# A hybrid FNet/Hyena encoder layer: z scaled behind later transposes, first spectra loaded during the filters, two units' spectra stored once and copied in DRAM

## The chip, the core and the metric

One Trainium2 chip, of which the kernel uses one core. A core has five engines with queues of their own: TensorE (PE: matrix products; its weight loads, PEld, run beside them), VectorE (DVE), ScalarE (ACT), GpSimd (POOL), and SyncE (SP), which here only starts DMA transfers. ACT starts some transfers too. Every queue is worked off in order; an instruction that waits holds all behind it on its engine. Engines wait for one another through semaphores. The metric is the device time of one launch in microseconds (us), lower is better.

## The reference, cut to what matters

```python
def reference(x, ...):                        # x: 1 x 2048 x 1024, float32, one layer
    h = rmsnorm(x, g_mix)
    p = h @ w_in                              # 1024 -> 2048 columns
    u_f, u_h = p[..., :512], p[..., 512:]
    y_f = rmsnorm(fourier_mix(u_f), g_fourier)     # Re(FFT2) over positions and 64 channels, 8 groups
    y_h = rmsnorm(hyena_mix(u_h, ...), g_hyena)
    x = x + concatenate([y_f, y_h]) @ w_out
    a = relu(rmsnorm(x, g_mlp) @ w_fc1) ** 2       # 1024 -> 4096
    return rmsnorm(x + a @ w_fc2, g_final)

def implicit_filters(...):                    # a small sine network over positions
    h = (hidden(positions) @ w_out) * decay   # 2 orders x 2 directions x 512 channels
    k = both directions joined to 4096 taps   # tap 0: forward + backward
    return k * rsqrt(sum(k * k) + EPS)

def hyena_mix(u, ...):
    x1, x2, v = split(short_conv(u))
    z = v
    for n, gate in enumerate((x1, x2)):       # rfft, product with the filter's spectrum, irfft
        z = gate * (irfft(rfft(z) * rfft(k[:, n])) + z * long_d[n])
    return z
```

## The kernel before

The stages follow each other: the input projections with short convolution (gates x1 and x2 until about 237 us, the Fourier group and v until about 408), `filters` (408 to 598, with the Fourier mixing in its first part), `hyena` (598 to about 800), the output projection, and the two large products of the MLP, which take more than half of the time. Matrix products of the projections and of the MLP are made in three passes over high and low parts. Transforms over positions are two stages of small matrix products with a DVE transpose between them.

**`filters` (L533).** Eight units `Unit(i)` make the spectra of eight filters of 128 channels: `ct = i // 2` is the channel block, `n = i % 2` the order. A loop of 44 steps (L675) is a pipeline over the units. Unit u multiplies out its taps in steps 4u to 4u+3: PE writes `pk` (L578), DVE multiplies by the decay into `k` (L583). For k = 0 ACT copies the tap in the middle to `lag0` (L592), DVE adds it to tap 0 (L593); for every k, ACT squares (L597) into `sqr` or, the first time, into `acc`, and POOL sums the squares (L599, folds L601, L602). In steps 4u+5 and 4u+6 the sum goes through PE (`psum_k`, L607) to the scales and to the skip term. The first stage of the transform is in steps 4u+7 to 4u+10 (PE L648, DVE transposes `Gk` L652), the second in 4u+12 to 4u+15 (PE L657, ACT copies into `ks` L660, and one store to DRAM a step, L664). A store writes the same 512 KB twice, for the two halves of the partitions of the later loads: 1024 KB. `ks` has three buffers.

In steps 0 to 10 the 16 first products of the Fourier mixing (L490, each followed by a DVE transpose `Gf`, L474) and then its 9 groups `rows(i)` (L494) are mixed in. `rows` makes the negative sines `neg` on ACT (L497) from the table `ff`; the table of the first group, `ff0`, is loaded at the start of the stage (L185). Of unit 0's four decay loads (L552), all are issued by ACT; those of later units by SP.

z, the input of the first Hyena order, is loaded from DRAM in steps 24 to 27 (L711) and multiplied by `norms`, the product of both orders' scales, from step 28 on (L715, 16 instructions). The framework's scheduler orders each engine's queue by priority, so instructions can stand earlier than the program text says.

**`hyena` (L719).** Eight blocks, first order (n = 0) of four channel blocks, then second order. A block takes `first` (PE L760, transposes), `second(q)` for eight q (PE L767, product with the spectrum `ks` on DVE and POOL, L773 to L775), `inverse` (PE L783), `turn`, `gate`; three blocks overlap. `spectrum(q)` (L737) loads 512 KB (L746); for q = 0 a small ACT copy moves row 64 (L749) and two POOL memsets clear two rows (L751). The first four spectra of block 0 are loaded at the stage's start (L805). Block i reads the unit with the same (n, ct): blocks 6 and 7 read units 5 and 7.

`behind(later, first)` (L202) puts instructions behind another one in the queue of the same engine, with no semaphore. `ordered` does that for PE, so that PE's order in the filters is that of the program text. A DMA takes one of eight semaphores in turn and is not issued before the transfer that had it last (eight transfers back) has landed.

The lines that matter in the order of the filters' loop are these:

```python
            if 0 < step < 32:
                units[u].generate(k)
...
            if 0 <= u < 8:
                units[u].stage1(r)
...
            if step in LOAD:
...
                nc.sync.dma_start(zzs[0][:, :, cs], gd[0][:, :, cs])
            j, q = divmod(step - 28, 4)
            if j >= 0:
                z = zzs[0][:, 4 * q : 4 * q + 4, 128 * j : 128 * j + 128]
                nc.vector.tensor_mul(z, z, norms[:, j : j + 1, :].broadcast_to([P, 4, 128]))
```

Of the kernel before, what the change touches and what calls it, by code (L numbers as in the profile page):

```python
# [134 lines left out]
def hybrid_block(ctx: ExitStack, tc: tile.TileContext, A, out):  # L135
# [203 lines left out]
    line = []  # L339
# [144 lines left out]
    def fourier(fp, uf, e1f, ffs):  # L484
# [8 lines left out]
        def rows(i):  # L493
# [3 lines left out]
            nc.scalar.mul(neg, ffs[i][:, :, 1], -1.0)  # L497
# [35 lines left out]
    def filters(ctx, tp, fp, gp, zp, zzs, norms, emb, wo, e1k, f2, dk8, tabs, fourier_steps):  # L533
# [7 lines left out]
        class Unit:  # L541
# [3 lines left out]
            def decay(self, k):  # L545

                if k < 2:
                    decs[k] = fp.tile([P, 8, 128], F32, tag="dec", name="dec", bufs=2)
                elif k == 2:
                    two = tp.tile([P, 2, 8, 128], F32, tag="dec2", name="dec2")  # L550
                    decs[2], decs[3] = two[:, 0], two[:, 1]
                d = (nc.scalar if self.i == 0 else nc.sync).dma_start(decs[k], A["decay"][self.ct][:, 8 * k : 8 * k + 8, :])  # L552
                if self.i == 0:
                    behind([d], line[0])
# [26 lines left out]
            def multiply(self, k, p, first=None):  # L581
# [7 lines left out]
                if k == 0:  # L589
                    zero, end = self.k[0:1, :, 0, :], self.k[32:33, :, 0, :]  # L590
                    lag0 = fp.tile([1, 128], F32, tag="lag0", name="lag0", bufs=2).rearrange("p (c j) -> p c j", c=8)
                    nc.scalar.copy(lag0, end)  # L592
                    nc.vector.tensor_add(zero, zero, lag0)  # L593
                    nc.vector.memset(end, 0.0)
# [43 lines left out]
            def stage1(self, r):  # L638
# [10 lines left out]
                for c in range(2):  # L649
                    src = p[:, :, 256 * c : 256 * c + 256].rearrange("p a (l c e) -> p c e a l", c=8, e=2)  # L650
                    dst = self.G.rearrange("p c (a f) e -> p c e a f", a=2)[:, 16 * r + 8 * c : 16 * r + 8 * c + 8]
                    nc.vector.transpose(dst, src)  # L652

            def stage2(self, q):
                p = pa("pk2")
                for j in range(4):
                    ordered(nc.tensor.matmul(p[:, 128 * j : 128 * j + 128], lhsT=f2[:, 4 * q + j, :], rhs=self.G[:, :, 4 * q + j], start=True, stop=True))  # L657
                if q % 2 == 0:
                    self.ks = sp[0].tile([P, 8, 128], F32, tag="ks", name="ks", bufs=3)
                nc.scalar.copy(self.ks[:, 4 * (q % 2) : 4 * (q % 2) + 4, :], p.rearrange("p (f c) -> p f c", f=4))  # L660
                if q % 2:

                    dst = kd[self.ct][self.n].rearrange("h p s x -> (p s) h x")[:, :, 512 * q - 512 : 512 * q + 512]
                    nc.sync.dma_start(dst, self.ks.rearrange("p (h f) c -> p h (f c)", h=1).broadcast_to([P, 2, 1024]))  # L664
# [9 lines left out]
        LOAD = {24: 0, 25: 1, 26: 2, 27: 3}  # L674
        for step in range(44):  # L675
# [21 lines left out]
            if 0 <= u < 8:  # L697
                units[u].stage1(r)
# [13 lines left out]
            j, q = divmod(step - 28, 4)  # L712
            if j >= 0:
                z = zzs[0][:, 4 * q : 4 * q + 4, 128 * j : 128 * j + 128]
                nc.vector.tensor_mul(z, z, norms[:, j : j + 1, :].broadcast_to([P, 4, 128]))  # L715
# [3 lines left out]
    def hyena(hp, wp, rp, zz, e1, b1, f2, a2, work):  # L719
# [6 lines left out]
        class Block:  # L726
# [9 lines left out]
            def spectrum(self, q):  # L736

                if self is blocks[7] and q > 3:
# [3 lines left out]
                    ks = self.room[:, q - 4]  # L742
                else:
                    ks = hp.tile([P, 2, 4, 128], F32, tag="ks", name="ks", bufs=4)
                src = kd[self.ct][self.n].rearrange("h p s x -> (h p) s x")[:, :, 512 * q : 512 * q + 512]
                nc.sync.dma_start(ks.rearrange("p s f c -> p s (f c)"), src)  # L746
# [58 lines left out]
        blocks = [Block(n, ct) for n in range(2) for ct in range(4)]  # L805
        for k in range(4):
            blocks[0].ahead[k] = blocks[0].spectrum(k)

# [3 lines left out]
        for i in range(8):  # L812
            cur, old, older, new = (blocks[j] if 0 <= j < 8 else None for j in (i, i - 1, i - 2, i + 1))
            for q in range(8):
# [28 lines left out]
                if new:  # L843
                    for c in FIRSTS[q]:
                        new.first(c)
        old, older = blocks[7], blocks[6]
# [705 lines left out]
```

## Time and profile before

| | us |
|---|---|
| three timed runs | 2271.7, 2274.6, 2276.61 |
| their median | 2274.6 |
| profiled execution | 2276.27 |
| its span in the trace | 2274.5 |
| PE busy in the span | 2204.1 |

Busy time by stage, from the windows of the trace:

| stage | window, us | PE | DVE | ACT | POOL | clock | DMA share |
|---|---|---|---|---|---|---|---|
| gates x1, x2 | 0 to 237 | 220.45 | 202.78 | 125.93 | 98.22 | 1.00 | 0.58 |
| Fourier group, v | 237 to 408 | 171.00 | 116.58 | 30.66 | 50.38 | 0.99 | 0.78 |
| filters | 408 to 598 | 172.82 | 123.46 | 88.08 | 83.50 | 0.96 | 0.77 |
| hyena | 598 to 800 | 195.20 | 154.31 | 118.91 | 125.14 | 0.99 | 0.79 |

A row of a timeline gives the start and the duration of an instruction (or of several like it, with their count after an x), the engine (ACTq and SPq are the queues that start transfers), the line, the operation, what is written and read, and in brackets the idle time before it with the instruction that ended it. A row of the waits gives the waiting instruction, what it waited for, the time in all, how often, and the longest. Clock is the share of TensorE's full clock that was granted; the DMA share is the busy share of the core's 16 DMA engines.

### The profile page before, as it was taken

To read this page: it belongs to the slowest core of one execution; us is meant where nothing else is said; L and a number is where in the kernel's file an instruction comes from. 1 tells how busy PE (TensorE), PEld (TensorE's weight loads), DVE (VectorE), ACT (ScalarE), POOL (GpSimd) and SP (SyncE) were. 2 spreads that over 40 slices of the span, in tenths; PEclk is the share of its full clock that TensorE was granted. 3 is DMA by queue.
4 is the path that set the end of the run, shared out by engine and by line. 5 is a ranking of instruction groups with operands and counts; after the bars stand their busy time and mean duration, and the time that the engine had idled before them with its cause. 6 is when DMAs were issued, how large, how long until landed. Compare 5 with 4: busy or idle time off the path is not lost.

```text
span 2274.5 us, 34533 instructions
## 1 busy us (share of the span) xinstructions
PE 2204.1 (97%) x12881; PEld 1800.7 (79%) x12881; DVE 1470.5 (65%) x2196; ACT 1074.3 (47%) x1788; POOL 768.9 (34%) x583
## 2 busy tenths in 40 slices
PE   8999899898999989998999999999999999999998
PEld 6888788576788858887888878888888888888886
DVE  6999667677487764456444466444466666866667
ACT  6545211354465654456555565555533333533333
POOL 3434232464276601246555556555300000000000
PEclk9999999999999999999999999999999999999999
DMA  8535887578977755657444474444498766866631
GB/s 272 177 134 173 297 300 256 188 257 305 368 247 219 235 158 167 199 181 247 158 153 151 152 249 167 153 153 152 140 352 324 241 194 194 305 191 197 188 119 74
DMA packets 296505, 477.00 MB, mean 210 GB/s; under 512 B 17349, under 2 KB 141455, under 8 KB 292113
## 3 DMA queue, kind: packets, MB, share of 16 engines
q1 hardware_dynamic: 290097, 458.29, 60.4%
q10 hardware_dynamic: 6240, 16.51, 2.1%
q8 instruction: 101, 1.65, 0.3%
q14 instruction: 67, 0.55, 0.1%
HBM read 305.17 MB, written 168.00 MB: 208 GB/s over the span
## 4 chain that ended last, share of the span: by engine, by line
PE 85%; DVE 4%; DMA 4%; ACT 3%; POOL 2%; issue 2%; ACTq 0%; SPq 0%; DVEq 0%; POOLq 0%
PE p2u L210 5%; PE p2u L212 5%; PE p2u L211 5%; PE p1u L212 5%; PE p1u L210 5%; PE p1u L211 5%; PE pu L212 4%; PE pu L211 4%; PE pu L210 4%; PE p2v L210 3%; PE p2v L212 3%; PE p2v L211 3%; PE pk L657 2%; PE p1v L210 2%; PE pz L760 2%; PE p1v L212 2%
## 5 line engine op out<-in xcount | busy, mean ns | idle before, releaser
L196 ACT CAST qahm<-ra 128x1024 fp32r<-128x1024 f32 x110 | 115.9, 1054 | 346.5 <-PE p2u L211 172.0
L197 DVE TENSOR_TENSOR qalm<-ra,qahm 128x1024 fp32r<-128x1024 f32 x110 | 134.7, 1224 | 153.7 <-ACT qahm L196 152.1
L1324 POOL TENSOR_TENSOR acc<-acc,gfin 128x512 f32<-128x512 f32 x4 | 5.1, 1278 | 631.6 <-DMA out<-acc 624.5
L211 PE MATMUL pu<-wl,xh 128*128 128x512 f32 x512 | 201.2, 393 | 6.9 <-DVE wl L197 6.5
L210 PE MATMUL pu<-wh,xh 128*128 128x512 f32 x512 | 203.7, 398 | 1.0 <-ACT wh L199 1.0
L212 PE MATMUL pu<-wh,xl 128*128 128x512 f32 x512 | 201.1, 393 | 1.5 <-DVE xl L197 1.5
L211 PE MATMUL p2u<-qblm,qahm 128*128 128x512 f32 x504 | 196.1, 389 | 0.0
L210 PE MATMUL p2u<-qbhm,qahm 128*128 128x512 f32 x504 | 195.8, 389 | 0.0
L212 PE MATMUL p2u<-qbhm,qalm 128*128 128x512 f32 x504 | 195.8, 389 | 0.0
L197 DVE TENSOR_TENSOR qblm<-rb,qbhm 128x1024 fp32r<-128x1024 f32 x110 | 134.0, 1218 | 1.1 <-ACT qbhm L196 0.9
L405 POOL TENSOR_TENSOR acc<-acc,cw 128x512 f32<-128x512 f32 x45 | 59.9, 1330 | 201.5 <-DVE acc L382 198.1
L196 ACT CAST ahm<-s 128x512 fp32r<-128x512 f32 x124 | 76.7, 621 | 98.5 <-PE p1v L211 53.7
L197 POOL TENSOR_TENSOR alm<-W,ahm 128x512 fp32r<-128x512 f32 x63 | 88.5, 1405 | 94.8 <-ACT ahm L196 94.8
L211 PEld LDWEIGHTS pu<-wl,xh 128*128 128x128 f32 x512 | 96.9, 189 | 28.5 <-DVE wl L197 6.9
L196 ACT CAST qbhm<-rb 128x1024 fp32r<-128x1024 f32 x110 | 115.3, 1049 | 3.3 <-DMA rb<-in_w_fc 2.1
L212 PEld LDWEIGHTS pu<-wh,xl 128*128 128x128 f32 x512 | 96.8, 189 | 22.9 <-DVE xl L197 3.0
L210 PEld LDWEIGHTS pu<-wh,xh 128*128 128x128 f32 x512 | 97.0, 189 | 22.2 <-ACT wh L199 1.8
L210 PEld LDWEIGHTS p2u<-qbhm,qahm 128*128 128x128 f32 x504 | 94.6, 188 | 20.1 <-issue 0.3
L212 PEld LDWEIGHTS p2u<-qbhm,qalm 128*128 128x128 f32 x504 | 94.6, 188 | 19.6
L211 PEld LDWEIGHTS p2u<-qblm,qahm 128*128 128x128 f32 x504 | 94.6, 188 | 19.6
L210 PE MATMUL p1u<-bm,ahm 128*128 128x512 f32 x252 | 99.5, 395 | 7.2 <-ACT ku L1186 7.2
L196 ACT CAST ahm<-W 128x512 fp32r<-128x512 f32 x94 | 57.7, 617 | 98.8 <-PE p1u L211 98.8
(376 smaller groups left out, 6153.3 us busy)
## 6 DMA issues: line engine op xcount, KB each, us to landing
W<-in_w_fc SPq DMA_DIRECT2D x66, 512.0 KB, 4.6
spec<-ks SPq DMA_DIRECT2D x32, 1024.0 KB, 5.7
ks<-spec SPq DMA_DIRECT2D x64, 512.0 KB, 4.7
rb<-td SPq DMA_DIRECT2D x64, 512.0 KB, 9.3
ra<-a1m SPq DMA_DIRECT2D x56, 512.0 KB, 3.6
ra<-a0m SPq DMA_DIRECT2D x54, 512.0 KB, 3.7
rb<-in_w_fc SPq DMA_DIRECT2D x46, 512.0 KB, 10.7
f<-in_w_fc SPq DMA_DIRECT2D x16, 1024.0 KB, 7.6
```

The lines of the kernel that those rows point to most:

```text
L196: nc.scalar.copy(hi, src)
L197: (eng or nc.vector).tensor_sub(lo, src, hi)
L210: a = nc.tensor.matmul(o, lhsT=lh, rhs=rh, start=start, stop=False, skip_group_check=more)
L211: nc.tensor.matmul(o, lhsT=lh, rhs=rl, start=False, stop=False, skip_group_check=more)
L212: return a, nc.tensor.matmul(o, lhsT=ll, rhs=rh, start=False, stop=stop, skip_group_check=more)
L405: nc.gpsimd.tensor_add(m1, m1, cw[:, 3, :])
L657: ordered(nc.tensor.matmul(p[:, 128 * j : 128 * j + 128], lhsT=f2[:, 4 * q + j, :], rhs=self.G[:, :, 4 * q + j], start=True, stop=True))
L760: nc.tensor.matmul(p[:, 256 * sp : 256 * sp + 256], lhsT=e1[:, sp, :], rhs=zz[:, :, lo : lo + 16], start=True, stop=True)
L1324: nc.gpsimd.tensor_mul(acc[i][:, c], acc[i][:, c], gfin[:, c])
```

## The change

There are five edits. (1) `neg` is put behind unit 0's lag copy in ACT's queue. (2) Of unit 0's decay loads the last two (`dec2`) are issued by SP instead of ACT. (3) z is scaled in steps 30 to 37, two instructions a step, and each is put behind the transposes of its step in DVE's queue. (4) The first four spectra of block 0 are loaded into a tile of their own, `ks4`, with a high priority and behind unit 3's last store in SP's queue, which is issued in step 27; the repair of q = 0 goes with them. (5) Units 5 and 7 store their spectra once (512 KB a store); the second half is written by eight copies from DRAM to DRAM, `doubled`, in blocks 1 and 2 of the hyena stage.

```diff
--- before.py
+++ after.py
@@ -336,7 +336,13 @@
                 w[h, k] = hi, lo
         return w
 
-    line = []
+    line, acts, fetched, stored = [], [], [], []
+    SINGLE = (5, 7)
+
+    def doubled(i, q):
+
+        both = kd[i // 2][i % 2].rearrange("h p s x -> h (p s) x")[:, :, 1024 * q : 1024 * q + 1024]
+        behind([nc.sync.dma_start(both[1], both[0])], fetched[0])
 
     def project(ip, fx, cps, sets, uf):
 
@@ -494,7 +500,7 @@
 
             n, p = len(groups[i]), pa("pf2")
             neg = fp.tile([P, 2, P], F32, tag="neg", name="neg", bufs=2)[:, 0:n]
-            nc.scalar.mul(neg, ffs[i][:, :, 1], -1.0)
+            behind([nc.scalar.mul(neg, ffs[i][:, :, 1], -1.0)], acts[0])
             for s, f in enumerate(groups[i]):
                 co, si, ns = ffs[i][:, s, 0], ffs[i][:, s, 1], neg[:, s]
                 a, b = p[:, 256 * s : 256 * s + 132], p[:, 256 * s + 132 : 256 * s + 256]
@@ -549,8 +555,8 @@
                 elif k == 2:
                     two = tp.tile([P, 2, 8, 128], F32, tag="dec2", name="dec2")
                     decs[2], decs[3] = two[:, 0], two[:, 1]
-                d = (nc.scalar if self.i == 0 else nc.sync).dma_start(decs[k], A["decay"][self.ct][:, 8 * k : 8 * k + 8, :])
-                if self.i == 0:
+                d = (nc.scalar if self.i == 0 and k < 2 else nc.sync).dma_start(decs[k], A["decay"][self.ct][:, 8 * k : 8 * k + 8, :])
+                if self.i == 0 and k < 2:
                     behind([d], line[0])
 
             def generate(self, k):
@@ -589,7 +595,7 @@
                 if k == 0:
                     zero, end = self.k[0:1, :, 0, :], self.k[32:33, :, 0, :]
                     lag0 = fp.tile([1, 128], F32, tag="lag0", name="lag0", bufs=2).rearrange("p (c j) -> p c j", c=8)
-                    nc.scalar.copy(lag0, end)
+                    acts.append(nc.scalar.copy(lag0, end))
                     nc.vector.tensor_add(zero, zero, lag0)
                     nc.vector.memset(end, 0.0)
                 for q in range(2):
@@ -649,7 +655,8 @@
                 for c in range(2):
                     src = p[:, :, 256 * c : 256 * c + 256].rearrange("p a (l c e) -> p c e a l", c=8, e=2)
                     dst = self.G.rearrange("p c (a f) e -> p c e a f", a=2)[:, 16 * r + 8 * c : 16 * r + 8 * c + 8]
-                    nc.vector.transpose(dst, src)
+                    last = nc.vector.transpose(dst, src)
+                return last
 
             def stage2(self, q):
                 p = pa("pk2")
@@ -660,8 +667,11 @@
                 nc.scalar.copy(self.ks[:, 4 * (q % 2) : 4 * (q % 2) + 4, :], p.rearrange("p (f c) -> p f c", f=4))
                 if q % 2:
 
-                    dst = kd[self.ct][self.n].rearrange("h p s x -> (p s) h x")[:, :, 512 * q - 512 : 512 * q + 512]
-                    nc.sync.dma_start(dst, self.ks.rearrange("p (h f) c -> p h (f c)", h=1).broadcast_to([P, 2, 1024]))
+                    n = 1 if self.i in SINGLE else 2
+                    dst = kd[self.ct][self.n][0:n].rearrange("h p s x -> (p s) h x")[:, :, 512 * q - 512 : 512 * q + 512]
+                    d = nc.sync.dma_start(dst, self.ks.rearrange("p (h f) c -> p h (f c)", h=1).broadcast_to([P, n, 1024]))
+                    if self.i == 3:
+                        stored[:] = [d]
 
         units = [Unit(i) for i in range(8)]
         decs, both, sp = {}, [], []
@@ -672,6 +682,7 @@
         SOLO = 11
         FOURIER = (4, 4, 4, 4, 2, 1, 1, 1, 1, 2, 1)
         LOAD = {24: 0, 25: 1, 26: 2, 27: 3}
+        SCALE = {30 + 2 * j + h: [(j, 2 * h), (j, 2 * h + 1)] for j in range(4) for h in range(2)}
         for step in range(44):
             if step == SOLO:
                 yield
@@ -695,7 +706,7 @@
                 units[u].generate(k)
             u, r = divmod(step - 7, 4)
             if 0 <= u < 8:
-                units[u].stage1(r)
+                flipped = units[u].stage1(r)
             u, q = divmod(step - 5, 4)
             if 0 <= u < 8 and q == 0:
                 units[u].scales()
@@ -709,10 +720,9 @@
                 if not zzs:
                     zzs.append(zp.tile([P, NT, 512], F32, tag="zz", name="zz"))
                 nc.sync.dma_start(zzs[0][:, :, cs], gd[0][:, :, cs])
-            j, q = divmod(step - 28, 4)
-            if j >= 0:
+            for j, q in SCALE.get(step, ()):
                 z = zzs[0][:, 4 * q : 4 * q + 4, 128 * j : 128 * j + 128]
-                nc.vector.tensor_mul(z, z, norms[:, j : j + 1, :].broadcast_to([P, 4, 128]))
+                behind([nc.vector.tensor_mul(z, z, norms[:, j : j + 1, :].broadcast_to([P, 4, 128]))], flipped)
         yield
 
 
@@ -740,10 +750,14 @@
                     if q == 4:
                         self.room = rp.tile([P, 4, 2, 4, 128], F32, tag="W", name="ks4")
                     ks = self.room[:, q - 4]
+                elif self is blocks[0] and q < 4:
+                    if q == 0:
+                        self.room = rp.tile([P, 4, 2, 4, 128], F32, tag="W", name="ks4")
+                    ks = self.room[:, q]
                 else:
                     ks = hp.tile([P, 2, 4, 128], F32, tag="ks", name="ks", bufs=4)
                 src = kd[self.ct][self.n].rearrange("h p s x -> (h p) s x")[:, :, 512 * q : 512 * q + 512]
-                nc.sync.dma_start(ks.rearrange("p s f c -> p s (f c)"), src)
+                fetched[:] = [nc.sync.dma_start(ks.rearrange("p s f c -> p s (f c)"), src)]
                 if q == 0:
 
                     nc.scalar.copy(ks[64:65, 0, 0, :], ks[64:65, 1, 0, :])
@@ -803,9 +817,11 @@
         LAST = ((0,), (1, 2), (3, 4), (5, 6), (7,))
         FIRSTS = ((0, 1), (2, 3), (4,), (5,), (6,), (7,), (), ())
         blocks = [Block(n, ct) for n in range(2) for ct in range(4)]
+        with tc.high_priority(offset=4000):
+            for k in range(4):
+                blocks[0].ahead[k] = blocks[0].spectrum(k)
+                behind(fetched, stored[0])
         for k in range(4):
-            blocks[0].ahead[k] = blocks[0].spectrum(k)
-
             nc.sync.dma_start(a2[:, 8 * k : 8 * k + 8], A["a2"][:, 8 * k : 8 * k + 8])
         for c in range(8):
             blocks[0].first(c)
@@ -843,6 +859,8 @@
                 if new:
                     for c in FIRSTS[q]:
                         new.first(c)
+                if i in (1, 2) and q % 2:
+                    doubled(SINGLE[i - 1], q // 2)
         old, older = blocks[7], blocks[6]
         for q in range(8 - LAG, 8):
             old.inverse(q)
```

PE's queue is the same in both programs. Three places of the other queues follow. In ACT's queue at the start of the filters before, the four loads of `dec` and `dec2` stand ahead of the copy of `longd`, and the two `neg` ahead of `lag`:

```order
L462 ACTIVATE uf<-pu_3563,nw_s 128x512
L552 DMA dec<-in_decay 128x1024 x2
L552 DMA dec_3622<-in_decay 128x1024 x2
L539 COPY longd<-plongd 128x8
L497 ACTIVATE neg<-ff_3612 128x128
L497 ACTIVATE neg<-ff 128x256
L592 COPY lag_3674<-k 1x128
L597 ACTIVATE sqr<-k 128x512
L597 ACTIVATE acc<-k 128x512
```

and of the change:

```order
L468 ACTIVATE uf<-pu_3563,nw_s 128x512
L558 DMA dec<-in_decay 128x1024 x2
L545 COPY longd<-plongd 128x8
L598 COPY lag_3674<-k 1x128
L603 ACTIVATE sqr<-k 128x512
L503 ACTIVATE neg<-ff_3612 128x128
L503 ACTIVATE neg<-ff 128x256
L603 ACTIVATE acc<-k 128x512
```

Two loads have left ACT, the lag copy and one square stand ahead of `neg`, and `acc`, which POOL's sums begin with, stands behind it.

In DVE's queue around step 24 the scaling of z (`zz<-zz,norms`) stood between the transposes `Gk` and the decay products `k` before (the last three rows are of step 24):

```order
L583 TENSOR_TENSOR k<-pk,dec_4723 128x8x8x16
L715 TENSOR_TENSOR zz<-zz,norms 128x4x128 x2
L652 STREAM_TRANSPOSE Gk<-pk_5319 128x8x2x32 x2
L715 TENSOR_TENSOR zz<-zz,norms 128x4x128 x2
L583 TENSOR_TENSOR k<-pk,dec 128x8x8x16
L593 TENSOR_TENSOR k<-k,lag_5380 1x8x16
```

In the change the same transposes (of `pk_5319`) have none beside them, and the first scaling stands in step 30, behind its transposes (the first two rows below):

```order
L658 STREAM_TRANSPOSE Gk<-pk_5833 128x8x2x32 x2
L725 TENSOR_TENSOR zz<-zz,norms 128x4x128 x2
L589 TENSOR_TENSOR k<-pk,dec_5307 128x8x8x16
L658 STREAM_TRANSPOSE Gk<-pk_5903 128x8x2x32 x2
L725 TENSOR_TENSOR zz<-zz,norms 128x4x128 x2
L658 STREAM_TRANSPOSE Gk<-pk_5930 128x8x2x32 x2
```

All 16 scalings have moved behind the transposes of steps 30 to 37. In SP's queue of the change, the four loads of the first spectra (`ks_6229`, the tile `ks4`) stand between the stores of unit 3 (`spec_63`) and those of unit 4 (`spec_64`); before, the first of them stood behind all stores:

```order
L672 DMA spec_63<-ks 128x2x1024
L722 DMA zz<-gates_57 128x16x128
L672 DMA spec_63<-ks 128x2x1024
L760 DMA ks_6229<-spec_60 128x2x512 x4
L672 DMA spec_64<-ks 128x2x1024 x4
L717 DMA f2h<-in_f 128x1024 x2
L672 DMA spec_65<-ks 128x1024
```

and ACT's queue of the change has the repair of q = 0 in step 28, between step 27's copies into `ks` and unit 7's lag copy:

```order
L667 COPY ks<-pk_5627 128x512
L667 COPY ks<-pk_5634 128x512
L763 COPY ks_6229<-ks_6229 1x128
L598 COPY lag_5677<-k 1x128
L603 ACTIVATE sqr<-k 128x512
```

So the repair has moved from the hyena stage ahead of unit 7's lag copy, and waits for its load there.

## The prediction

> **What bounds the kernel now.** I read the page's busy shares first, then the waits of PE alone over the filters and the first hyena block (405 to 640 us), since the change touches nothing outside that stretch but loads.
>
> ```profile
> span 2274.5 us, 34533 instructions
> PE 2204.1 (97%) x12881; PEld 1800.7 (79%) x12881; DVE 1470.5 (65%) x2196; ACT 1074.3 (47%) x1788; POOL 768.9 (34%) x583
> ```
> ```profile
> PE pk L648 <- DVE Gk L652: 7.5, 2, 4.6
> PE pv L783 <- POOL y L775: 3.5, 1, 3.5
> PE pf L490 <- ACT longd L539: 3.5, 1, 3.5
> PE pf L490 <- DVE Gf L474: 2.0, 1, 2.0
> ```
>
> PE works 97% of the span, so the change can win only what PE idles, plus what it loses at a slow clock behind an idle spell. The four waits above (16.5 us together) are the places. They lie at three points: the filters' start, steps 24 to 28, and the first hyena block. PE's own order of work is the same before and after, so each wait that goes moves everything behind it forward, until the next engine is late.
>
> **A, the filters' start (`neg` and two decay loads).** The timelines of PE, ACT and POOL, and one row of the chain of waits:
>
> ```profile
> 410.42 5.42 PE L490 MATMUL pf<-uf,e1f 128*128 128x512 f32 x12
> 419.29 3.63 PE L490 MATMUL pf<-uf,e1f 128*128 128x512 f32 x4 [3.45 <-ACT longd L539]
> ...
> 430.94 3.70 PE L490 MATMUL pf<-uf,e1f 128*128 128x512 f32 x8
> ...
> 435.66 0.49 PE L504 MATMUL pf<-Gf,ff 128*128 128x132 f32 x2
> ...
> 441.92 0.38 PE L607 MATMUL psum_k<-ones,acc 128*128 128x1 f32 x2 [0.66 <-POOL acc L602]
> ```
> ```profile
> 408.65 10.38 ACTq L552 DMA_DIRECT2D dec<-in_decay  x4
> 419.07 0.17 ACT L539 COPY longd<-plongd 128x8 f32<-128x8 f32 x1 [9.79 <-DMA gates<-last]
> 424.81 0.61 ACT L497 ACTIVATE neg<-ff 128x128 f32<-128x128 f32 x2 [5.57 <-DMA ff<-in_ff]
> 425.45 0.30 ACT L592 COPY lag<-k 1x128 f32<-1x128 f32 x1
> ```
> ```profile
> 418.09 6.65 DMA ff<-in_ff
> ```
> ```profile
> 427.02 1.27 POOL L599 TENSOR_TENSOR acc<-acc,sqr 128x512 f32<-128x512 f32 x1 [17.98 <-ACT acc L597]
> ...
> 441.41 0.46 POOL L602 TENSOR_TENSOR acc<-acc 128x128 f32<-128x128 f32 x1
> ```
>
> ACT issues four decay loads; the last two are held until 419.03, and the small `longd` copy stands behind them, so PE waits 3.45. Then `neg` waits for `ff` until 424.81, and the lag copy behind it keeps DVE, hence PE, for 2.02 more. With two loads left on ACT and the lag copy ahead of `neg`, both go. PE is through with its first 12 matmuls at 410.42 + 5.42 = 415.84. Up to L504 it has 20 more (the rows of 4, 2, 6 and 8) at 3.63/8 = 0.454 us, by the eight that begin at 430.94 and end with the next start at 434.57, and three `pk` groups at some 1.08: 9.1 + 3.2 = 12.3, so L504 starts near 428.2 instead of 435.66, 7.5 earlier. That is the two waits (5.47) and the half-speed row of 419.29 (3.63 for four instead of 1.82, so 1.8). What is late next is POOL: its seven sums and two folds take 7 x 1.3 + 0.73 + 0.47 = 10.3 us and can begin only behind ACT's `acc`, which now stands behind `neg`. If `ff` lands no earlier than 424.74, POOL starts at about 426.1 and ends at 436.4, where PE, 7.5 earlier, would want it at 434.4: 2 us given back. But `ff` now waits for an older store and has no decay loads beside it, so it should land some 1 to 3 us earlier. I take **-7.0**; ends -8 (all) and -4 (POOL's late start and a later `ff`).
>
> The two moved decay loads (512 KB each) are issued on SP in the projections, some 150 us earlier. SP passes them ahead of a weight load; PE shows no wait there between 236.9 and 408, so **0**, at most +2 if that weight load, first used at 250.8, is late by the two loads' 2.8 us.
>
> **B, steps 24 to 31 (scaling of z, early spectra).** PE, DVE and SP timelines, the one store in the window 544 to 545 us, and two 10-us windows (busy PE, PEld, DVE, ACT, POOL, then clock, DMA share, GB/s):
>
> ```profile
> 505.79 1.16 PE L578 MATMUL pk<-wo,emb 64*32 64x128 f32 x64
> ...
> 522.23 1.16 PE L578 MATMUL pk<-wo,emb 64*32 64x128 f32 x64
> 528.03 1.63 PE L648 MATMUL pk<-k,e1k 64*32 64x512 f32 x16 [4.64 <-DVE Gk L652]
> 529.59 3.12 PE L657 MATMUL pk<-Gk,f 128*128 128x128 f32 x16
> ...
> 534.71 2.05 PE L657 MATMUL pk<-Gk,f 128*128 128x128 f32 x16
> ...
> 551.73 1.44 PE L578 MATMUL pk<-wo,emb 64*32 64x128 f32 x64
> 552.91 1.12 PE L648 MATMUL pk<-k,e1k 64*32 64x512 f32 x16
> ```
> ```profile
> 525.11 1.55 DVE L715 TENSOR_TENSOR zz<-zz,norms 128x512 f32<-128x512 f32 x2 [4.37 <-DMA zz<-gates]
> ...
> 554.81 0.28 DVE L593 TENSOR_TENSOR k<-k,lag 1x128 f32<-1x128 f32 x1 [0.36 <-ACT lag L592]
> ```
> ```profile
> 544.30 21.32 SPq L664 DMA_DIRECT2D spec<-ks  x5
> ```
> ```profile
> spec<-ks SPq DMA_DIRECT2D x1, 1024.0 KB, 7.1
> ```
> ```profile
> 530.00:540.00 10.00, 10.00 (x203) 7.62 (x202) 8.49 (x18) 5.53 (x13) 4.17 (x3) 0.91 1.06 319
> ...
> 560.00:570.00 10.00, 10.00 (x217) 6.79 (x217) 5.89 (x9) 6.27 (x13) 7.21 (x6) 1.00 0.71 247
> ```
>
> Before, DVE stands in its queue at the z scaling until z's loads land, and the transposes behind it are late. Steps 20 to 24 take 16.44 us, steps 24 to 28 take 29.50: 13.1 us lost in waits and slow clock. Moving the scaling removes all of that. But the change adds a wait in the same place: the load of the first spectra stands on SP right behind unit 3's last store (the one issued at 544.30), and the small ACT copy that repairs its row 64 stands in step 28 directly ahead of unit 7's lag copy. Behind that copy wait DVE's add, the transposes behind the add on DVE, and PE. The DMA share of 1.06 says that the engines are full with z (4 MB) and the stores, with or without the scaling, so the store lands at 544.30 + 7.1 = 551.4 in either case (on the clock of before; A shifts both alike). A 512 KB load behind it takes 0.524 MB / 368 GB/s = 1.4 us (the rate at a full share, quoted under D): 552.8. Copy and lag copy at 0.3 each put DVE's add at 553.5, against 554.81 before: -1.3. Without the hold, PE would bring the add 3.1 us after a `pk` at 522.23 + 16.44, at 541.8; so PE now idles some 10 us, and starts again slowly. After the 4.64 gap the two rows of 528.03 and 529.59 took 4.75 instead of 1.12 + 2.05: 1.6 lost. Sum **+0.3**. Ends: -12 if the load is not late (13.1 less a remaining us), and +5.4 if the store takes 8.9, as the one in the window 523 to 524.2 did, and the load its usual 4.7. The scaling itself (16 of 0.8 us, 13 us) goes to steps 30 to 37 behind that step's transposes, where DVE was 59% busy: nothing, at most 0.6.
>
> The Trainium skill, "TensorE: Matmul & The Clock Gate", section "Part 1: The HAM clock gate", gives half rate after an idle window of about 3.4 us, and full rate after about 3.4 us of work, however long the idle spell: an estimate of 1.7 us for the new 10 us gap, where the rows give 1.6.
>
> **C, the first hyena block.** PE and SP timelines, and the chain of waits:
>
> ```profile
> 616.91 1.85 PE L783 MATMUL pv<-y,f 128*128 128x128 f32 x8 [3.46 <-POOL y L775]
> 618.55 1.91 PE L760 MATMUL pz<-zz,e1z 128*128 128x256 f32 x4
> ...
> 622.22 1.03 PE L760 MATMUL pz<-zz,e1z 128*128 128x256 f32 x4
> ```
> ```profile
> 604.38 3.15 SPq L746 DMA_DIRECT2D ks<-spec  x3
> ```
> ```profile
> 606.62 7.65 DMA ks<-spec
> ```
>
> The first spectra are asked for at 604.38 and reach POOL at 614.27. Loaded in step 28, they are there, and POOL's two operations of 1.27 follow PE's first transforms (607.3) by more than PE needs. The 3.46 goes, and the slow rows behind it (1.85 and 1.91 instead of 1.05 and 1.03, some 1.85 with the next): **-5.3**; ends -5.5 and -1, if the next loads become late instead.
>
> **D, stores and copies.** Two windows, one 10-us window at a full share, and the page's row:
>
> ```profile
> 610.00:620.00 10.00, 6.54 (x36) 5.90 (x35) 4.39 (x7) 5.57 (x10) 5.99 (x7) 0.86 1.00 368
> ```
> ```profile
> 600.00:650.00 50.00, 46.54 (x316) 43.46 (x315) 31.65 (x50) 26.52 (x47) 30.09 (x29) 0.97 0.93 314
> 650.00:700.00 50.00, 50.00 (x355) 42.99 (x354) 43.17 (x67) 29.41 (x51) 32.06 (x29) 1.00 0.71 212
> ```
> ```profile
> spec<-ks SPq DMA_DIRECT2D x32, 1024.0 KB, 5.7
> ```
>
> Eight stores are halved: 8 x 1.4 = 11.4 us of DMA time saved while PE is not waiting for them. Eight copies of 512 KB within DRAM come back in blocks 1 and 2 (about 623 to 673). No row shows such a copy: between 1.4 us of the engines each (as a load) and 2.8 (read and write counted apart), 11.4 to 22.8 in all. Spare are 7% of 50 us, 29% of the 25 from 650 on, and the 11.4 saved: 22.1. So 0 to +0.7; I take **+0.5**, upper end +3.5, a wait like the one of C once more.
>
> The Trainium skill, "DMA: Bandwidth & Descriptors", section "Latency and other measured facts", has 207 to 214 GB/s per direction for copies between tensors in HBM. By it a copy is an estimated 2.45 us, eight are 19.6, and D would be 0; no run here shows one yet.
>
> **Sum.** -7.0 + 0.3 - 5.3 + 0.5 = -11.5. Against the profiled run's 2276.27 (its span of 2274.5 and 1.8 around it) that is 2264.8; against the median of 2274.6 shown (the profiled run lies 1.7 above it), **2263.1**, which I predict.
>
> **Rivals.**
> - The scaling pays in full, because z and the stores drain faster without the hold or the load of the spectra overtakes. For it: the scaling's wait did cost 13.1. Against: the share of 1.06. B is -12, the time 2250.8. Chance 0.12.
> - The hold in step 28 is longer (store 8.9, load 4.7): B +5.4, time 2268.2. Chance 0.10.
> - The change does only part of what it says: `ff` and POOL keep the start (-4), other loads come late at the hyena instead (-1): -4 + 0.3 - 1 + 0.5 = -4.2, time 2270.4. Chance 0.12.
> - Slower: the copies run one at a time and take the queue 5.7 us each, like a 1 MB store from issue to landing. 8 x 5.7 = 45.6, less 22.1 spare, makes the spectra of blocks 1 and 2 late by 23.5, and the sum -11.5 + 23.5 = +12: 2286.6. It decides from (22.1 + 11.5 + 4.5)/8 = 4.8 us a copy; at 2.8 it does nothing. Chance 0.05.
>
> **How the numbers follow.** The forecast has the remaining 0.61. Its own bounds (A to -4 or -8, D to +3.5) reach 2262 to 2269; with the second and third rival the range goes to 2272, and downward, part of the first rival taken in, to 2254. About 0.2% (4.5 us) is what a measurement here can tell from no change. Faster than 2270.1: the forecast, the first two rivals, a little of the third, 0.83. Same: most of the third, 0.11. Slower: the copies and unseen mishaps, 0.06.
>
> **What would show it.** Right: no PE wait on `longd`, L504 near 428, POOL's first sum before 426; a PE wait of about 10 us on DVE's transposes in step 28 or 29, released through the lag copy by the early load; no PE wait on `y` in the first block; blocks 1 and 2 at 25 us each. Wrong: steps 24 to 28 followed by step 28 without a wait (first rival), PE waits in blocks 1 and 2 (the last), or a PE wait for `psum_k` over 2 us (A too large).

## The result

| | before | changed |
|---|---|---|
| median of 8 runs each, us | 2274.37 | 2268.43 |
| lowest and highest, us | 2270.5, 2278.08 | 2264.99, 2270.66 |
| ratio of the changed kernel to the one before | | 0.9974 (95% interval 0.9963 to 0.9985) |
| span of the profiled execution, us | 2274.5 | 2268.0 |

The change saves 5.9 us, half of the 11.5 forecast. The page of the changed kernel has the same busy PE in a shorter span:

```profile
span 2268.0 us, 34541 instructions
...
PE 2200.2 (97%) x12881; PEld 1799.0 (79%) x12881; DVE 1474.9 (65%) x2196; ACT 1075.2 (47%) x1788; POOL 767.3 (34%) x583
```

The four waits that were to go have gone. The longest that PE has now over the same stretch are others (400 to 640 us; engine, line and what it waited for: us in total, times, longest):

```profile
PE psum_k L613 <- POOL acc L608: 5.7, 2, 3.3
PE pk L654 <- DVE vk L615: 5.4, 1, 5.4
PE pk L584 <- issue: 2.8, 2, 1.4
PE pk L654 <- issue: 1.8, 1, 1.8
```

PE's order is the same in both programs, so the start of the same instruction can be subtracted. The table does that at some places, each less the shift of unit 0's first `pk` (before 409.33, changed 408.60), because traces differ by up to 2 us ahead of the filters. Negative is earlier than before.

| place (start before, us) | changed | what lies between |
|---|---|---|
| L504, first group's rows (435.66) | -7.7 | the two waits at the start |
| unit 1's first `pk` behind `psum_k` (442.24) | -4.9 | a wait for POOL |
| step 20 (505.79) | -4.3 | half clock behind that wait, in part made up |
| step 28 (551.73) | -14.0 | the z scaling out of the way |
| step 30 (560.60) | -3.5 | the hold by the early load, and two gaps of 1.4 |
| the filters' end: first product of the hyena stage (598.28) | -0.6 | a second wait for POOL |
| first hyena block (622.22) | -6.0 | the wait for the first spectra |
| late in fc2 (2150.10) | -5.8 | blocks 1 and 2, and all the rest |

**The filters' start.** PE, ACT and POOL of the changed kernel:

```profile
427.27 0.49 PE L510 MATMUL pf<-Gf,ff 128*128 128x132 f32 x2
...
436.13 0.58 PE L613 MATMUL psum_k<-ones,acc 128*128 128x1 f32 x2 [3.27 <-POOL acc L608]
```
```profile
417.06 0.63 ACT L603 ACTIVATE sqr<-k 128x512 f32<-128x512 f32 x1
424.03 0.62 ACT L503 ACTIVATE neg<-ff 128x128 f32<-128x128 f32 x2 [6.34 <-issue]
424.56 0.61 ACT L603 ACTIVATE acc<-k 128x512 f32<-128x512 f32 x1
```
```profile
425.25 9.43 POOL L605 TENSOR_TENSOR acc<-acc,sqr 128x512 f32<-128x512 f32 x7 [16.93 <-ACT acc L603]
```

The lag copy is free, but `neg` still waits for its table `ff` (6.34 of idle time, to which the row gives no releaser; before, the same row named the load) and now holds ACT's `acc`. So POOL's seven sums run back to back from 425.25 without a gap, and PE, which is 7.7 earlier, waits 3.27 for them.

**Step 28.** SP, ACT, DVE and PE of the changed kernel:

```profile
541.03 3.77 SPq L760 DMA_DIRECT2D ks<-spec  x4
```
```profile
548.35 0.29 ACT L763 COPY ks<-ks 1x128 f32<-1x128 f32 x1 [10.68 <-DMA ks<-spec]
548.66 0.30 ACT L598 COPY lag<-k 1x128 f32<-1x128 f32 x1
```
```profile
548.99 0.28 DVE L599 TENSOR_TENSOR k<-k,lag 1x128 f32<-1x128 f32 x1 [7.87 <-ACT lag L598]
```
```profile
550.99 1.96 PE L654 MATMUL pk<-k,e1k 64*32 64x512 f32 x16 [5.38 <-DVE vk L615]
552.89 2.94 PE L664 MATMUL pk<-Gk,f 128*128 128x128 f32 x16
```

The repair of q = 0 stands idle for 10.68 us and keeps unit 7's lag copy, DVE's add and everything behind it. The name at PE (`vk`) is only the last of DVE's instructions that came late; DVE's own row names the cause. The products behind the wait run slowly again (1.96 and 2.94 against 1.12 and 2.05).

**Unit 7's sums.** DVE and PE a few steps later:

```profile
559.96 3.25 DVE L725 TENSOR_TENSOR zz<-zz,norms 128x512 f32<-128x512 f32 x2
563.13 1.21 DVE L589 TENSOR_TENSOR k<-pk,dec 128x1024 f32<-128x1024 f32 x1
...
565.51 3.20 DVE L725 TENSOR_TENSOR zz<-zz,norms 128x512 f32<-128x512 f32 x2
...
569.87 1.24 DVE L725 TENSOR_TENSOR zz<-zz,norms 128x512 f32<-128x512 f32 x2
```
```profile
569.89 0.38 PE L613 MATMUL psum_k<-ones,acc 128*128 128x1 f32 x2 [2.43 <-POOL acc L608]
```

The first pair of scalings stands ahead of unit 7's last decay product (563.13). It takes 3.25 us, as does the second; the third takes 1.24. The product, its squares and POOL's sums are late, and PE waits 2.43.

### The profile page after: what moved, and what is told of

Same layout as the page of the kernel before. It is cut to its first block, busy times and chain, and to the rows that moved or that the text cites. A ratio compares the mean times of both kernels' runs of the same rounds, so it can differ in the third digit from the quotient of the medians.

```text
span 2268.0 us, 34541 instructions
## 1 busy us (share of the span) xinstructions
PE 2200.2 (97%) x12881; PEld 1799.0 (79%) x12881; DVE 1474.9 (65%) x2196; ACT 1075.2 (47%) x1788; POOL 767.3 (34%) x583
## 4 chain that ended last, share of the span: by engine, by line
PE 86%; DVE 5%; ACT 2%; DMA 2%; POOL 2%; issue 2%; SPq 0%; ACTq 0%; DVEq 0%; POOLq 0%
PE p2u L210 5%; PE p2u L211 5%; PE p2u L212 5%; PE p1u L210 5%; PE p1u L212 5%; PE p1u L211 5%; PE pu L212 4%; PE pu L211 4%; PE pu L210 4%; PE p2v L210 3%; PE p2v L211 3%; PE p2v L212 3%; PE pz L781 2%; PE pz L774 2%; PE pv L797 2%; PE p1v L210 2%
## 5 line engine op out<-in xcount | busy, mean ns | idle before, releaser
L788 POOL TENSOR_TENSOR zs<-zs,ks 128x512 f32<-128x512 f32 x64 | 83.3, 1302 | 82.2 <-ACT zs L785 75.7
```

The source lines that it names most:

```text
L788: nc.gpsimd.tensor_mul(zs, zs, ks[:, 1])
```

## The experiments

All ratios are to the kernel before, run beside each kernel on the same chip, with a 95% interval. The last columns give shifts of the profiled execution as in the table above.

| run | ratio | interval | step 20 | step 28 | step 30 | filters' end | first block |
|---|---|---|---|---|---|---|---|
| the change | 0.9974 | 0.9963 to 0.9985 | -4.3 | -14.0 | -3.5 | -0.6 | -6.0 |
| e1 repair late | 0.9938 | 0.9921 to 0.9955 | -6.5 | -16.8 | -14.2 | -10.4 | -15.8 |
| e2 neg behind squares | 0.9964 | 0.9953 to 0.9975 | -8.0 | -18.6 | -7.5 | -3.6 | -9.0 |
| e3 scale from 32 | 0.9959 | 0.9945 to 0.9974 | -7.9 | -17.9 | -6.6 | -6.2 | -11.6 |
| e4 no early load | 0.9933 | 0.9916 to 0.9951 | -4.2 | -11.2 | -10.3 | -7.4 | -12.8 |
| e5 three edits | 0.9922 | 0.9909 to 0.9936 | -8.1 | -15.4 | -14.1 | -12.8 | -18.2 |
| e7 later scaling alone | 0.9984 | 0.9971 to 0.9997 | 0.1 | -7.0 | -5.6 | -1.7 | -2.5 |
| e8 no early load, all stores doubled | 0.9954 | 0.9941 to 0.9967 | -7.6 | -17.5 | -14.8 | -11.9 | -14.0 |
| e9 e4 with neg and scaling late | 0.9918 | 0.9906 to 0.9930 | -7.9 | -14.3 | -13.3 | -12.6 | -17.8 |
| e10 e9 with z loaded later | 0.9920 | 0.9907 to 0.9934 | -6.2 | -17.1 | -17.4 | -13.7 | -18.6 |
| e11 e9 with four units stored once | 0.9905 | 0.9890 to 0.9921 | -8.3 | -18.4 | -18.6 | -18.2 | -23.6 |

**e1: the repair behind unit 7.** The early loads stay.

```diff
-                    nc.scalar.copy(ks[64:65, 0, 0, :], ks[64:65, 1, 0, :])
-                    for h in (0, 64):
-                        nc.gpsimd.memset(ks[h : h + 1, 1, 0, :], 0.0)
+                    copied = nc.scalar.copy(ks[64:65, 0, 0, :], ks[64:65, 1, 0, :])
+                    cleared = [nc.gpsimd.memset(ks[h : h + 1, 1, 0, :], 0.0) for h in (0, 64)]
+                    if self is blocks[0]:
+                        behind([copied], done["act"])
+                        behind(cleared, done["pool"])
```

> The changed kernel with one edit: the early loads stay where they are, but the repair of q = 0 (ACT copy, two POOL memsets) stands behind unit 7's last square on ACT and its last fold on POOL. Theory: the 10.7 us that PE falls back in steps 28 to 30 of the changed kernel come from the repair that waits ahead of unit 7's lag copy. Then the wait of 5.4 on DVE before the first-stage product at 550.99 goes, PE passes steps 28 to 31 at about 4.1 us a step, and the time is about 8 us less than the changed kernel's 2268.4, so 2260; not the whole 10.7, because ks has three buffers and the stores are backed up. Rival: the stores' backlog holds PE at that place anyway (ACT's copies into ks wait for a landed store); then 2266 to 2268.

Measured 0.9938, 0.0036 below the change: 8 us. ACT's lag copy of unit 7 follows its product at once:

```profile
537.76 0.30 ACT L598 COPY lag<-k 1x128 f32<-1x128 f32 x1 [3.21 <-DVE k L589]
...
554.55 0.30 ACT L763 COPY ks<-ks 1x128 f32<-1x128 f32 x1
```

From step 28 to step 30 PE falls back 2.6 instead of 10.5. The hold was the repair; the rival (the stores hold PE there anyway) falls. Two gaps of PE are left in that stretch (1.1 each; more on such gaps under e10 and e11).

**e2: neg behind unit 0's squares of k = 1.**

```diff
-                    acts.append(nc.scalar.copy(lag0, end))
+                    nc.scalar.copy(lag0, end)
...
-                    nc.scalar.square(sq..., new[:, 4 * q : 4 * q + 4])
+                    made = nc.scalar.square(sq..., new[:, 4 * q : 4 * q + 4])
+                    if self.i == 0 and k == 1:
+                        acts[:] = [made]
```

> The changed kernel with one edit: neg stands behind unit 0's squares of k = 1 instead of its lag copy. Theory: in the changed kernel POOL's seven sums start only at 425.25, because ACT's acc stands behind neg, which waits for ff; PE then waits 3.3 us for psum_k and runs at half clock behind it, 4.9 given back in all. With POOL starting at about 418, L613 comes without a wait, and the time is 4 to 5 us less than 2268.4: 2264. Rival: what is won there is lost again at step 28, because the early load lands when the DMA engines are through with z and the stores, not earlier; then 2267 to 2268.4.

POOL starts at 416.61, with gaps between its sums, and PE waits as little for `psum_k` as before the change:

```profile
416.61 1.28 POOL L607 TENSOR_TENSOR acc<-acc,sqr 128x512 f32<-128x512 f32 x1 [8.94 <-ACT acc L603]
```
```profile
433.14 0.38 PE L615 MATMUL psum_k<-ones,acc 128*128 128x1 f32 x2 [0.66 <-POOL acc L610]
```

At step 20 the trace is 3.7 earlier than the changed kernel's, at the first hyena block 3.1, so little of it is lost at step 28. In the timed ratio it is 0.0010, 2 us, less than expected, and the intervals overlap. The rows of the other runs tell why: e3 and e8, which leave the start as the change has it, are at -7.9 and -7.6 by step 20, e1 at -6.5, e4 at -4.2. Counted from unit 0's first `pk`, their first `neg` starts at 13.4, 12.5, 14.2 and 15.1 us, that of the changed kernel at 15.4. When `ff` lands, and so how long POOL keeps PE, differs from one profiled execution to the next; the edit takes a loss away that comes in some of them only.

**e3: scaling from step 32.**

```diff
-        SCALE = {30 + 2 * j + h: ...
+        SCALE = {32 + 2 * j + h: ...
```

> The changed kernel with one edit: z is scaled in steps 32 to 39 instead of 30 to 37. Theory: the scalings of steps 30 and 31 (3.2 us a pair beside POOL's sums) stand on DVE ahead of unit 7's last decay product, so its squares, POOL's sums and psum_k are late: PE waits 2.4 and 0.6 us there. Without them both go: 3 us less than 2268.4, 2265.4. Rival: unit 7's sums are late because of the hold in step 28; then no change.

Measured 0.9959, 0.0015 below the change, 3.4 us, with intervals that overlap; the trace is clear: from step 30 to the filters' end PE loses 0.35 (by the unrounded shifts) instead of 2.9. `psum_k` of unit 7 waits 0.68, as unit 0's did before the change. The hold of step 28 is still there in e3, so the rival falls. Of the two pairs that the expectation puts ahead of unit 7's last product, only the first stands there (559.96 above); the second stands behind it, beside POOL's last two sums.

```profile
566.23 0.38 PE L613 MATMUL psum_k<-ones,acc 128*128 128x1 f32 x2 [0.68 <-POOL acc L608]
```

**e4 and e8: without the early load; and with all stores doubled again.** e4 loads the first four spectra where the kernel before did. e8 is e4 with `SINGLE = ()` and no copies, so that only `neg`, the two decay loads and the later scaling are left.

```diff
-        with tc.high_priority(offset=4000):
-            for k in range(4):
-                blocks[0].ahead[k] = blocks[0].spectrum(k)
-                behind(fetched, stored[0])
         for k in range(4):
+            blocks[0].ahead[k] = blocks[0].spectrum(k)
...
```

> The changed kernel with the first four spectra loaded at the hyena stage's start, as before the change. Theory: without the early load nothing holds unit 7's lag copy, so the gain of the moved scaling (10 us by step 28) stays, and the wait for the first spectra at the hyena stage comes back (5.4 with its slow clock): 4 to 5 us less than the changed kernel, 2264. Rival: the stores' backlog holds PE in steps 28 to 31 in place of the load; then 5 us more than the changed kernel, 2273.

> The changed kernel without the early load and with all stores doubled as before the change (no copies in DRAM): what is left is neg, the two decay loads and the later scaling. Theory: in the run without the early load the wait of 3.5 us in the first hyena block stayed away because the halved stores had cleared SP's queue some 7 us earlier, not because of an early load. With the stores doubled again PE waits 3 to 4 us for y there, and the ratio to before is 0.995 to 0.996, some 5 us worse than without the early load alone (0.9933). Rival: the wait is gone for another reason (the stage begins at another time); then 0.993 to 0.994 and no wait on y.

e4 measured 0.9933, some 9 us faster than the change, twice what was expected: the hold is gone, and the wait in the first block did not come back. e8 measured 0.9954, and there it did. The first `inverse` product of e8, then of e4:

```profile
604.36 1.16 PE L793 MATMUL pv<-y,f 128*128 128x128 f32 x8 [3.02 <-POOL y L785]
```
```profile
606.40 1.05 PE L793 MATMUL pv<-y,f 128*128 128x128 f32 x8
```

So halving units 5 and 7's stores is enough for the first spectra to be in time. Counted from the filters' end, SP asks for the first of them at 6.1 to 6.2 us where all stores are doubled (before, e7 and e8) and at 3.6 to 3.8 in e4 and e9, and it lands at 13.7 to 14.3 or at 10.5 to 10.7. That is 2.5 us earlier in the queue, not the 7 that the expectation of e8 names. From the filters' end to the first block e4 gains 5.4, as the change with its early load does; e8 gains 2.1.

There is a price behind that place, in the same block. Block 1's repair stands on ACT ahead of the copies `V` and waits for its own load, and PE waits for `V`. ACT and PE of e9:

```profile
611.99 0.29 ACT L761 COPY ks<-ks 1x128 f32<-1x128 f32 x1 [3.83 <-DMA ks<-spec]
```
```profile
614.23 1.13 PE L795 MATMUL pv<-y,f 128*128 128x128 f32 x8 [1.49 <-ACT V L796]
```

That repair waits 3.0 to 3.8 in e4, e8, e9 and e10, and at most 0.5 in the five kernels with the early load. From the place of the table's first block (622.22 before) to 647 us the five kernels without the early load fall back 1.0 to 1.9, those with it 0.0 to 0.5.

**e5 and e9: the edits together, with and without the early load.** e5 is the change with the edits of e1, e2 and e3, e9 the change with those of e4, e2 and e3.

> The changed kernel with the three edits of the runs so far: repair behind unit 7's squares and sums, neg behind unit 0's squares of k = 1, z scaled from step 32. Theory: the three losses (hold in step 28, POOL's late start, unit 7's late sums) are separate and add: the repair's 8, some 2 to 3 of neg, 3 of the scaling, so 0.9974 - 0.0036 - 0.0012 - 0.0014 = 0.991 of before. Rival: in steps 24 to 31 the DMA engines set the pace once the hold is gone, and what neg wins ahead of them is lost: then 0.9925 or above, the ratio of the repair alone less the scaling's part.

> The changed kernel without the early load, with neg behind unit 0's squares of k = 1 and z scaled from step 32; the halved stores and the copies stay. Theory: the early load brings nothing that the halved stores have not brought, so this is as fast as the version with three edits that keeps the load: 0.991 of before, no PE wait on y in the first hyena block. Rival: the load is worth something there; then some 3 us slower than that version.

0.9922 and 0.9918: the times can't be told apart. In the first block's wait for `y` the early load brings nothing that the halved stores have not brought; the 1 to 2 us that it is worth just behind, by the traces, are too few for the timed runs. The 0.991 that was expected lies within both intervals, so whether the three edits add up stays open; e5's trace has gaps of 2.7 and 1.3 without a releaser (below).

**e7: the later scaling alone, on the kernel before.** Edit (3) of the change and nothing else:

```diff
+        SCALE = {30 + 2 * j + h: [(j, 2 * h), (j, 2 * h + 1)] for j in range(4) for h in range(2)}
...
-            j, q = divmod(step - 28, 4)
-            if j >= 0:
+            for j, q in SCALE.get(step, ()):
...
-                nc.vector.tensor_mul(z, z, ...)
+                behind([nc.vector.tensor_mul(z, z, ...)], flipped)
```

> The kernel before with the later scaling of z alone. Theory: PE passes steps 24 to 28 without waiting for DVE, 10 us earlier (the trace of the changed kernel: shift -5.0 to -15.0), and nothing holds step 28; 3 us come back at unit 7's sums, behind the scalings of steps 30 and 31; the waits at the filters' start and in the first hyena block stay: 0.997 of before, 7 us. Rival: the DMA backlog of z and the stores keeps PE as long in steps 28 to 31, so that the 10 us are lost there: 1.000.

0.9984, half of what was expected: 7 us at step 28, not 10, and by the filters' end most of it is given back (-1.7), 1.4 up to step 30 and 3.8 behind it, most of that at unit 7's sums.

**e10 and e11: gaps without a releaser.** Where DVE no longer holds PE, PE has gaps that end with nothing in the profile ("issue"), in the middle of groups of equal products: in step 25 behind the fourth of 16 (the third in e7). In e7 that gap is 3.0, in the changed kernel 1.8, in e9 3.3. e10 loads z behind unit 4's stores in steps 28 to 31; e11 stores units 1 and 3 once too, with copies in blocks 0 to 3. Both build on e9.

```diff
-        LOAD = {24: 0, 25: 1, 26: 2, 27: 3}
+        LOAD = {28: 0, 29: 1, 30: 2, 31: 3}
...
-                    if self.i == 3:
-                        stored[:] = [d]
+                    stored[:] = [d]
...
-                nc.sync.dma_start(zzs[0][:, :, cs], gd[0][:, :, cs])
+                behind([nc.sync.dma_start(zzs[0][:, :, cs], gd[0][:, :, cs])], stored[0])
```

```diff
-    SINGLE = (5, 7)
+    SINGLE = (1, 3, 5, 7)
...
-                if i in (1, 2) and q % 2:
-                    doubled(SINGLE[i - 1], q // 2)
+                if i < 4 and q % 2:
+                    doubled(SINGLE[i], q // 2)
```

> The version without the early load, with neg and the scaling later, and with one more edit: z is loaded behind unit 4's stores in steps 28 to 31 instead of among unit 3's in steps 24 to 27. It looks at PE's gaps that end with no releaser, at the same three instructions of steps 25, 28 and 29 in all kernels in which DVE does not hold PE there (1.8 to 3.3 us for the first). Theory: PE waits for its instructions, which come in pieces of 16 KB over the same DMA engines and are late while z and the stores fill them. With z moved, the DMA share in steps 24 to 27 falls below 1.0, the gap of step 25 goes (below 0.5 us) and the gaps move to steps 28 to 32. Rival: the gap belongs to that place in the program (something in PE's queue); then it stays at 2 us or more at the same instruction. The time is 0.990 to 0.993 of before either way, so the trace decides.

> The version without the early load, with neg and the scaling later, and with units 1 and 3 stored once as well (16 copies in DRAM, in blocks 0 to 3). Theory: the copies cost nothing where PE does not wait for DMA, and each halved store takes 1.4 us of DMA time out of the filters; 5.7 us of them in steps 24 to 27, where the engines are full. Then PE's gap without a releaser in step 25 falls from 3.3 to 1 us or less, the hyena blocks stay at 25 us each, and the time is 0.990 of before. Rival: the copies in block 0 stand on SP among the first spectra and make them late; then PE waits for y in blocks 0 or 1, and it is 0.992 or more.

The gap of step 25 in e9, e10 and e11:

```profile
523.87 1.08 PE L656 MATMUL pk<-k,e1k 64*32 64x512 f32 x12 [3.29 <-issue]
```
```profile
522.25 1.08 PE L656 MATMUL pk<-k,e1k 64*32 64x512 f32 x12 [0.74 <-issue]
```
```profile
520.56 1.08 PE L656 MATMUL pk<-k,e1k 64*32 64x512 f32 x12 [1.56 <-issue]
```

and the window 520 to 530 us of e9 and of e10, whose last numbers are clock, DMA share and GB/s:

```profile
520.00:530.00 10.00, 6.71 (x76) 4.43 (x78) 3.45 (x8) 3.24 (x7) 2.58 (x3) 0.83 1.02 339
```
```profile
520.00:530.00 10.00, 9.26 (x184) 5.99 (x166) 6.32 (x14) 5.00 (x12) 3.82 (x4) 1.00 0.80 319
```

With z moved the gap is 0.7 instead of 3.3, at the same instruction, and the slow clock behind it goes. But the lighter traffic need not be the reason: e2 and e8 leave z where it was, their DMA share in the 10 us up to the gap's end is 1.06 and 1.05, and their gap is 0.8. Over the eleven kernels it is anything from 0.7 to 3.3. Nor did the gap go below 0.5 or move to steps 28 to 32, where the share of e10 is 1.10, as its theory had it; it did not stay at 2 or more either, as the rival had it. In e11 1 us or less was expected, and it is 1.6.

More is settled by a queue that the traces list beside the kernel's own transfers, as "instruction". It carries 101 packets of 16,384 bytes in the changed kernel. In the eleven traces with the later scaling, the gaps without a releaser of over 0.7 us in steps 25, 28 and 29 are 25, and each of them ends 1.2 to 1.6 us after such a packet has landed (in e9 a packet lands at 522.50 and PE goes on at 523.87). So the gaps are best read as PE waiting for its instructions. Why a packet comes late in one kernel and less late in another, no run tells.

e10 wins nothing in time (0.9920), because it loses 3.7 between step 30 and the filters' end. e11 has the lowest ratio of all: 0.9905, 2253.26 us, beside 2274.24 of the kernel before, with an interval that overlaps that of e9. From 580 to 720 us, where its first hyena blocks and their copies lie, PE waits once, for 0.6, so the rival (late spectra) falls.

## Why the prediction was right in sign and range, and about twice too large

The measured 2268.4 lies 5.3 us above the forecast and almost on the time of the second rival (2268.2). That is a coincidence: its longer hold did not come, and the missing gain lies in A and in a place that the sum put at nothing. The sign named for a too large A, a PE wait for `psum_k` of over 2 us, did come (3.27).

**A, the filters' start: too large in the profiled execution.** The two waits went, and the 7.5 earlier at L504 was met (7.7). "What is late next is POOL" was right, and so was its place. Its price was not: 2 us given back were weighed against an `ff` that "should land some 1 to 3 us earlier", and -7.0 was taken. In the profiled run `neg` started at 424.03 against 424.81, no earlier than the whole stage. PE waited 3.27 for `psum_k`, which gave 2.6 back, and the slow clock behind that new wait, left out of the sum, 0.8 more by step 20. The term was -4.3 in that execution, and between -4.2 and -7.9 in the other runs that have it as it is. In three of these, e1, e3 and e8, `neg` was 1.2, 2.0 and 3.0 earlier than before, as the forecast had it, and the term -6.5, -7.9 and -7.6. So -7.0 was a fair size where `ff` is early; what was missing is the execution in which it is not, which the end of -4 and the third rival named.

**B, steps 24 to 31: the mechanism right, both its parts too large.** The forecast was 13.1 won and 13.4 lost to the hold by the repair: +0.3. Measured were 9.8 won (step 20 to 28) and 10.5 lost (step 28 to 30): +0.8 by the unrounded shifts. e1 shows the hold to be the repair. The 13.1 fell short because a wait that nothing hides any more appeared in its place: the gap without a releaser in step 25, 1.8 long, at which PE falls back 2.4; the remaining 0.9 is not accounted for. Both parts shrank by about the same, 3.3 and 2.9, because the end of the hold is set by the load and not by PE. DVE's add behind it came 0.8 earlier than before, beside the shift of step 20, where 1.3 was forecast. What PE loses ahead of the hold only makes the wait at the hold shorter. The first rival (the scaling pays in full) needed the load to be in time; e7 shows that even without any early load the scaling alone brought 7 us at step 28, not 12, in an execution with a gap of 3.0 in step 25.

**The scaling's new place: wrong.** "Nothing, at most 0.6", because DVE was 59% busy there. It cost 2.9 (step 30 to the filters' end), and e3 takes 2.6 of that away. The share did not say that the first pair stands ahead of unit 7's last product, whose sums PE waits for, nor that a pair takes 3.2 us beside POOL's sums, where it takes 1.24 alone.

**C, the first hyena block: the size right, the cause given not needed.** -5.3 was forecast, -5.4 came. But e4 has the same gain without the early load, and e8, with all stores doubled, has not. The halved stores, which D counted only as room on the DMA engines, are enough for it. Whether the early load alone would be enough too, no run tells, since none has it with all stores doubled. What it is worth beside the halved stores is the 1 to 2 us in the rest of the first block, and it costs the 8 us of the hold.

**D, the copies: nothing,** as the lower end had it. From the first block to fc2 the changed kernel keeps its shift (-6.0, -5.8). The rival that the copies make the kernel slower did not occur, in e11 with sixteen of them either, although a copy took 7.0 us from issue to landing (median of the eight), more than the 5.7 and the 4.8 that the rival reckoned with. So the time to a copy's landing is not time that it takes from the other transfers; a copy's own price stays open.

The sum by the trace is -4.3 + 0.8 + 2.9 - 5.4 + 0.2 = -5.8, against -11.5: 2.7 of the difference is A, 2.9 the scaling.

## What to carry to other kernels

When a small instruction that waits for a transfer is put early in an in-order queue, look at what stands behind it on that engine: here an ACT copy of one row cost some 8 us (e1). A wait that is removed shows the next one in the same place, so check the sums of a slower engine (POOL here) and the instructions that are now ahead of the last one of a chain. And try each part of a change without the others: with the stores halved, the early load was not needed for the wait that it was meant for.

## What the runs showed of the hardware

A pair of scalings on DVE (two operands in SBUF) takes 3.2 us while POOL sums and 1.24 us alone; two of POOL's sums take 2.96 to 2.98 us beside such a pair and 2.64 without (e3). The Trainium skill, "SBUF — State Buffer", section "SBUF: two separate sides", says that such a DVE operation and a GpSimd operation take turns at a shared pair of ports and block each other; the trace agrees.

PE's gap without a releaser in step 25 lies at the same instruction (in e7 one before it) in the eleven kernels in which DVE does not hold PE there, 0.7 to 3.3 us long. This gap and the others of over 0.7 us behind it end 1.2 to 1.6 us after a packet of 16,384 bytes has landed on the queue marked "instruction", in 25 gaps of 25. The Trainium skill, "Runtime: NRT & Kernel Launch", section "Instruction fetch mechanics", has instructions fetched in blocks of 16 KiB over a DMA queue of the sequencer's own, at a cost that is mostly hidden. The packets here have that size, but gaps of up to 3.3 us are not hidden. That a full DMA makes the packets late is not shown: the gap was 0.8 in e2 and e8 at a share of 1.06 and 1.05, and 0.7 in e10 with z moved away.
